# Raw blocks of the output projection's weight sums in idle buffers, and the T1 splits of a Strassen product behind the last head, in a one-core attention and recurrence trunk

## The chip, the cores and the metric

The kernel runs on one core of a Trainium2 chip. The metric is the device time of one execution in microseconds (us). The engines are PE (matrix products; PEld is its weight loading), DVE (vector), ACT (scalar), POOL (GpSimd) and SP, which here only issues transfers.

## The reference

1024 tokens of width 1024 go through two layers. Each has a mixer and a SwiGLU channel mixer, both behind an RMS norm that is shifted and scaled by a conditioning vector (adaLN). Layer 0 mixes by forgetting attention, layer 1 by gated linear attention (GLA), here a recurrence of four heads over eight blocks of 128 tokens:

```python
for i in range(DEPTH):
    mod = c_act @ ada_w[i] + ada_b[i]
    sh1, sc1, g1, sh2, sc2, g2 = jnp.split(mod, N_MOD, axis=-1)
    h = modulate(rms_norm(x, norm1_g[i]), sh1, sc1)
    ...                                   # y: attention (i = 0) or GLA (i = 1)
    x = x + g1[:, None, :] * y
    h = modulate(rms_norm(x, norm2_g[i]), sh2, sc2)
    x = x + g2[:, None, :] * swiglu(h, ffn_w_in[i], ffn_w_out[i])
return rms_norm(x, final_g)

# GLA, per head: state S, decay alpha, q, k, v, gate r
o = o_intra + o_inter                     # A (lower triangle) times v, and q_in times the state before
o = o * lax.rsqrt(jnp.mean(o * o, axis=-1, keepdims=True) + EPS)
o = (o * g_o * silu(r)) ; y = o @ w_out
```

## The kernel before

**Arithmetic.** Every fp32 product is three matrix products of halves. A `split` makes the halves: ACT casts the value to the high part (L174), DVE subtracts it from the value (L175) for the low part. `mm3` issues the three products (L305 to L307). Weights come raw by SP into a ring `wr` of three slots (s16, s17, s18), are split by ACT (L242) and by POOL and DVE (L246), and go on into the ring `ws`.

**Order.** The program is written as generators that are interleaved (`weave`), and each engine's order is then fixed by a scheduler. `tc.issue_after(i)` and `behind_all()` add an order without a wait: what stands under them comes behind instruction i on its engine. `split_after` holds, for each engine, the instruction behind which weight splits and everything under `behind_all()` go.

**The GLA layer** lies at 1280 to 1672 us of the profile. Per head: the k and q projections (`gk`, `gq`), the intra product masked by `atz` and split as `ahl`, the state products `kv`, the state `Sf` and its split `S_t`, the output `go`, its norm (`junk` on ACT, `gss` on DVE and POOL), `on_t` on DVE, its transpose `ogt` on PE and the gate product into `gs` (L2128). `gs` lies in a ring `gsr` of two slots (s47 and s31) and is stored to `og_d` behind each head but the last. Behind a head's recurrence `gv_body` makes the next head's v (`gvt`, slots s48, s49, s53 and s25). Beside all of this `ada1` makes the second channel mixer's conditioning from 64 KB pieces of `ada_w` (`ad`, L442 to load, L505 on DVE), which SP loads in between.

**The output projection** is a Strassen product with seven terms (B11, T1, T2, T3, T4, B21, B22). On the weight side the blocks a11, a12, a21, a22 of `gla_w_out` are added up on POOL by `ow_sums(g)`, for one of four column groups per head, and stored to DRAM as `ow` 5, 7, 6 and 3. On the activation side, with a = `og_t[j]` and c = `og_t[4 + j]` and their halves 0 and 1, T1 = a0 − a1, T2 = c0 − T1 and T3 = c0 − a0. For j = 0 and 1 T2 and T3 are made early; for j = 2 and 3, made of the third and fourth heads, they are made in `out_blocks`, during the last head. Each is split into a `goT` or `goB` tile (`goT23` is T2 for j = 3). The four accumulators `oc0` to `oc3` take B11, T2 and T3 in turn; between them `out_add` (x on DVE, L2302) reads each into the residual, and PE can't go on to the next term in that bank before.

**The channel mixers** (`ffn`, both layers) work in four groups i of two residual tiles each. Behind the last part of a group five additions (on POOL for the first three groups, on DVE for the fourth) and four gate products on DVE finish it.

Of the kernel before, what the change touches and what calls it, by code (L numbers as in the profile page):

```python
# [16 lines left out]
P = 128  # L17
# [36 lines left out]
def trunk(ctx, tc, x, c, ada_w, ada_b, norm1_g, norm2_g, ffn_w_in, ffn_w_out,  # L54
# [910 lines left out]

    def ow_sums(g):

        raw = [wr([P, 2, 4, P], F32, f"pw{g}") for _ in range(2)]
        for i in range(2):
            for j in range(2):  # L970
                nc.sync.dma_start(raw[i][:, j], ow_src(g, (i, j)))
        (a11, a12), (a21, a22) = ((r[:, 0], r[:, 1]) for r in raw)
        yield
        nc.gpsimd.tensor_add(a22, a21, a22)
        yield
        nc.gpsimd.tensor_sub(a21, a11, a21)
        yield
        nc.gpsimd.tensor_sub(a11, a22, a11)
        yield
        nc.gpsimd.tensor_sub(a12, a12, a11)  # L980
        for nm_, r in ((5, a22), (7, a21), (6, a11), (3, a12)):
            d = ow_d[(nm_, g)] = tc.dram_tile([P, 4, P], F32, name=f"ow{nm_}{g}")
            nc.sync.dma_start(d, r)

    OW = [(nm_, g) for nm_ in (1, 6, 7, 5, 3, 2, 4) for g in range(4)]
# [486 lines left out]
    def ffn(l, oh, xs, slots, nm, mid, norm_end, each=None, blocks=None):  # L1472
# [289 lines left out]

        hp, xr, zs, ends = {}, {}, {}, deque()

# [55 lines left out]
        for c_ in range(OC):  # L1820
# [3 lines left out]
            for i in range(4):  # L1824
# [6 lines left out]
                def p_(j):  # L1831
                    ps = prod(feed.next(), o[c_][ONAMES[j]])
                    if last:
                        advance(i + 1 if j else i)
                        if i == 3:
                            advance(8)
                        if j == 2:
                            load_xr(i)
                    elif i < 3:
                        advance(NSP * (7 * i + j + 1) // 21)  # L1840
                    elif j:
                        advance(min(NSP + 3 * j, 7 * OD))
                    return ps
# [23 lines left out]
                fins = [lambda: V.tensor_add(Y1, Y1, Z1), lambda: V.tensor_add(Y4, Y4, Z1),  # L1867
                        lambda: V.tensor_sub(Y2, Y4, Y2), lambda: V.tensor_add(Y4, Y4, Z5),
                        lambda: V.tensor_sub(Y3, Y4, Y3)]
                gates_ = [lambda a=a, hf=hf, v_=v_: gated(a, hf, v_)  # L1870
                          for (a, hf), v_ in (((0, 0), Y1), ((1, 0), Y2), ((1, 1), Y4), ((0, 1), Y3))]
                if i < 3:
                    for f in fins + gates_:
                        f()
                else:
                    ends.extend([fins[0], gates_[0], fins[1], fins[2], gates_[1], None, fins[3], None, fins[4], None,
                                 gates_[2], None, gates_[3]])
# [118 lines left out]

    def gv_body(h, wv, tp):

        ps = pj([P, 2, 256], F32, f"gv{h}{tp}")
        for i in range(2):  # L2000
            run(proj_tok(ps[:, i, :], wv, h1, 2 * tp + i))
        ada1(5.1)
        v = vr([P, 2, 2, 256], FR, f"gvt{h}{tp}")
        split(v[:, 0], v[:, 1], ps)
# [40 lines left out]

    def head_front(h, b16, t2, ei, nmid):


        wk = feed.next()
        sums = ow_sums(h)  # L2050
        next(sums)
        kin = Pair(kir([P, S], FR, f"kih{h}"), kir([P, S], FR, f"kil{h}"))
        for hf in range(2):
# [4 lines left out]
            ada1(5.1)  # L2058
            next(sums)
            y = yv()  # L2060
# [8 lines left out]
        for hf in range(2):  # L2069
# [9 lines left out]
        return kin, qt  # L2079

    def head_back(h, kin, qt, t2, dec, vt, gs, need):
# [53 lines left out]
        for g in range(2):  # L2135
# [6 lines left out]
            for half in range(2):  # L2142
# [19 lines left out]
                for i2 in range(2):  # L2162
                    nc.vector.tensor_scalar(on_t[:, half, i2], o[:, i2, :], sst[:, i2:i2 + 1], None, op0=ALU.mult)
                yield 0.01
            yield from og_out(g)
# [21 lines left out]
    vt = []  # L2187
# [120 lines left out]
    def out_blocks(views):  # L2308
# [9 lines left out]
        for j in (2, 3):  # L2318
            a, c_ = og_t[j], og_t[4 + j]
            nc.gpsimd.tensor_sub(a[:, h1_], a[:, h0_], a[:, h1_])  # L2320
            ob_split("T1", j, a[:, h1_])
            nc.vector.tensor_sub(a[:, h1_], c_[:, h0_], a[:, h1_])
# [139 lines left out]
```

## Time and profile before

| | us |
|---|---|
| time, median of 3 runs (lowest to highest) | 2371.12 (2369.95 to 2371.66) |
| the profiled execution's own time | 2371.09 |
| its span in the trace | 2369.4 |
| PE busy | 2343.2 |
| DVE busy | 1787.3 |
| ACT busy | 1121.9 |
| POOL busy | 1104.7 |

All times within the execution are counted from the start of the span. Busy time is how long an engine worked on its instructions; an engine's idle time costs something only where PE then waits. A row of the timeline gives start, length, engine, line, operation, output and inputs, shape and count, and in brackets the idle time ahead of it and what ended it.

### The profile page before, as it was taken

Reading aid. Unit: us, or ns where it says so; the run is one execution under the profiler, and the core shown is the slowest. Engines: PE = TensorE matmul, PEld = TensorE weight load, DVE = VectorE, ACT = ScalarE, POOL = GpSimd, SP = SyncE. Lnnn points to the kernel's source line nnn. Section 1 sums busy time; section 2 is a strip of 40 time slices with the busy share of each in tenths; the row PEclk is TensorE's granted clock in tenths of the full one; section 3 lists DMA queues with packets and bytes.
Section 4 is the critical chain, followed back from the end, with each engine's and each line's share of the span. In section 5 each row is a group of like instructions: output and inputs, shape, how many; then the busy total and the mean of one; then the engine's idle time right before and its main releaser. Section 6 shows DMA issues by size and latency. Waiting matters only on the chain.

```text
span 2369.4 us, 35786 instructions
## 1 busy us (share of the span) xinstructions
PE 2343.2 (99%) x12208; PEld 1993.9 (84%) x12208; DVE 1787.3 (75%) x2994; ACT 1121.9 (47%) x2186; POOL 1104.7 (47%) x995
## 2 busy tenths in 40 slices
PE   8999999999999999999999999999999999999999
PEld 7888888888888888888888899887888888888888
DVE  6577787886688888876788665668787777875787
ACT  6556566665443333345325644344444333345326
POOL 1334444533445665653363432245356665643262
PEclk9999999999999999999999999999999999999999
DMA  8423333332435555457665453454434544457664
GB/s 259 148 77 114 105 121 94 121 126 98 142 103 168 187 165 168 163 195 256 227 210 165 132 148 110 118 185 161 138 106 163 178 147 151 147 200 257 226 201 150
DMA packets 349998, 375.00 MB, mean 158 GB/s; under 512 B 25756, under 2 KB 287032, under 8 KB 349816
## 3 DMA queue, kind: packets, MB, share of 16 engines
q1 hardware_dynamic: 349816, 372.72, 47.9%
q8 instruction: 96, 1.57, 0.3%
q14 instruction: 86, 0.70, 0.1%
HBM read 275.56 MB, written 97.06 MB: 157 GB/s over the span
## 4 chain that ended last, share of the span: by engine, by line
PE 83%; DVE 7%; DMA 3%; issue 2%; POOL 2%; ACT 2%; SPq 1%; DVEq 0%; POOLq 0%; ACTq 0%
PE p_b L305 15%; PE p_b L307 15%; PE p_b L306 15%; PE o_b L1305 2%; PE t_b L1291 2%; PE qk_b L305 2%; PE qk_b L306 2%; PE qk_b L307 2%; PE vps_b L307 1%; PE vps_b L305 1%; PE vps_b L306 1%; PE s_b L1259 1%; PE s_b L1260 1%; PE gr_b L305 1%; PE gr_b L306 1%
## 5 line engine op out<-in xcount | busy, mean ns | idle before, releaser
L175 DVE TENSOR_TENSOR o_s<-xv_s,o_s 128x512 fp32r<-128x512 f32 (+1 forms) x376 | 322.9, 863 | 57.3 <-ACT o_s L174 57.0
L174 ACT CAST o_s<-xv_s 128x512 fp32r<-128x512 f32 (+1 forms) x376 | 216.6, 587 | 297.3 <-PE p_b L307 249.3
L307 PE MATMUL p_b<-B,o_s 128*128 128x512 f32 x608 | 236.0, 389 | 0.0
L306 PE MATMUL p_b<-B,o_s 128*128 128x512 f32 x608 | 235.9, 389 | 0.0
L305 PE MATMUL p_b<-B,o_s 128*128 128x512 f32 x608 | 235.4, 390 | 0.0
L918 POOL TENSOR_TENSOR ex_s<-xv_s,xv_s 128x512 f32<-128x512 f32 (+1 forms) x64 | 90.8, 1419 | 284.2 <-DMA xv_s<-in_ffn_w_in_dram 118.0
L1271 POOL TENSOR_SCALAR lp_s<-lp_s,st 128x128 f32<-128x128 f32 (+7 forms) x128 | 98.0, 769 | 246.6 <-DVE st L1270 230.4
L305 PE MATMUL p_b<-T,o_s 128*128 128x512 f32 x480 | 186.9, 389 | 0.0
L306 PE MATMUL p_b<-T,o_s 128*128 128x512 f32 x480 | 186.8, 389 | 0.0
L307 PE MATMUL p_b<-T,o_s 128*128 128x512 f32 x480 | 181.2, 389 | 0.0
L307 PEld LDWEIGHTS p_b<-B,o_s 128*128 128x128 f32 x608 | 114.1, 188 | 23.9
L305 PEld LDWEIGHTS p_b<-B,o_s 128*128 128x128 f32 x608 | 114.1, 188 | 23.7 <-DVE x L1636 0.2
L306 PEld LDWEIGHTS p_b<-B,o_s 128*128 128x128 f32 x608 | 114.1, 188 | 23.5
L1269 ACT ACTIVATE lp_s<-lp_s,st 128x128 f32<-128x128 f32 (+7 forms) x128 | 99.4, 777 | 58.5 <-DVE st L1265 57.2
L246 POOL TENSOR_TENSOR w_l_s<-w__s,w_h_s 128x256 fp32r<-128x256 f32 x90 | 71.7, 824 | 100.1 <-ACT w_h_s L242 69.2
L920 POOL TENSOR_TENSOR xv_s<-ex_s,xv_s 128x512 f32<-128x512 f32 (+1 forms) x64 | 87.1, 1362 | 63.3 <-DVE o_s L175 61.1
L174 ACT CAST pt_s<-t_b 128x512 fp32r<-128x512 f32 (+1 forms) x160 | 79.7, 547 | 72.6 <-PE t_b L1291 72.0
L1636 DVE TENSOR_TENSOR ex_s<-ex_s,p_b 128x512 f32<-128x512 f32 x140 | 93.6, 680 | 20.7 <-PE p_b L307 20.6
L175 DVE TENSOR_TENSOR pt_s<-t_b,pt_s 128x512 fp32r<-128x512 f32 (+1 forms) x160 | 96.2, 630 | 15.9 <-ACT pt_s L174 15.4
L307 PEld LDWEIGHTS p_b<-T,o_s 128*128 128x128 f32 x480 | 90.1, 188 | 18.7
L306 PEld LDWEIGHTS p_b<-T,o_s 128*128 128x128 f32 x480 | 90.1, 188 | 18.6
L305 PEld LDWEIGHTS p_b<-T,o_s 128*128 128x128 f32 x480 | 90.1, 188 | 18.6
(1803 smaller groups left out, 7438.0 us busy)
## 6 DMA issues: line engine op xcount, KB each, us to landing
xv_s<-in_ffn_w_in_dram SPq DMA_DIRECT2D x176, 256.0 KB, 3.2
hid_B<-x SPq DMA_DIRECT2D x70, 512.0 KB, 3.0
ad_s<-in_ada_w_dram SPq DMA_DIRECT2D x384, 64.0 KB, 2.3
hid_T<-x SPq DMA_DIRECT2D x36, 512.0 KB, 2.9
xv_s<-in_ffn_w_out_dram SPq DMA_DIRECT2D x96, 192.0 KB, 4.8
ada_s<-in_ada_w_dram SPq DMA_DIRECT2D x96, 128.0 KB, 2.8
xv_s<-in_ffn_w_out_dram SPq DMA_DIRECT2D x40, 256.0 KB, 2.9
T2o<-hid_T SPq DMA_DIRECT2D x18, 512.0 KB, 8.3
```

The source lines that it names most:

```text
L174: nc.scalar.copy(hi, src)
L175: nc.vector.tensor_sub(lo, src, hi.bitcast(F32))
L246: (nc.gpsimd if i < 3 else nc.vector).tensor_sub(lo[:, cs], rw[:, cs], hi[:, cs].bitcast(F32))
L305: nc.tensor.matmul(ps, ah, bh, start=start, stop=False, skip_group_check=chain)
L306: nc.tensor.matmul(ps, ah, bl, start=False, stop=False, skip_group_check=chain)
L307: nc.tensor.matmul(ps, al, bh, start=False, stop=stop, skip_group_check=chain)
L918: nc.gpsimd.tensor_add(s1, a21, a22)
L920: nc.gpsimd.tensor_sub(a11, s1, a11)
L1269: nc.scalar.activation(lp, lp, AF.Exp, bias=mcur, scale=-1.0, accum_out=st[:, qi, 2:3])
L1271: nc.gpsimd.tensor_scalar(lp, lp, st[:, qi, 3:4], 1.0, op0=ALU.mult, op1=ALU.mult)
L1291: nc.tensor.transpose(tp[:, i, :], lps[qi][:, psl(2 * b + jj)], ident)
L1636: nc.vector.tensor_add(d, d if src is None else dest(G, src), ps)
```

## The change

**Weight sums.** `ow_sums` takes its raw blocks from a ring that is handed in instead of from `wr`: for the first head from `qr` (slots of the q tiles, not in use yet), and for the others from `gsr`, the two slots that the head before has just stored to `og_d`. It is started earlier: ahead of the first head, or in `gv_body` of the head before. Each raw block comes by one load of 512 KB instead of two, and the sums go back by two stores of 512 KB instead of four of 256 KB.

**Last head.** T3 is made first (on POOL), T2 = T3 + a1 behind it (on DVE), and T1 as c0 − T2, later. T1's splits, and the other splits under `behind_all()`, now go behind `on_last`, the last ACT and DVE instructions that made `on_t`.

**Channel mixers.** The third group's additions and gates are collected in `pend` and called two at a time behind the products of the fourth group, and the residual of the fourth group is loaded two products later.

```diff
-    def ow_sums(g):
-        raw = [wr([P, 2, 4, P], F32, f"pw{g}") for _ in range(2)]
+    def ow_sums(g, ring):
+        raw = [ring([P, 2, 4, P], F32, f"pw{g}") for _ in range(2)]
         for i in range(2):
-            for j in range(2):
-                nc.sync.dma_start(raw[i][:, j], ow_src(g, (i, j)))
+            nc.sync.dma_start(raw[i].rearrange("p j k m -> p (j k) m"),
+                              gla_w_out[0][:, psl(2 * g + i)].rearrange("(k p) m -> p k m", p=P))
...
-        for nm_, r in ((5, a22), (7, a21), (6, a11), (3, a12)):
-            d = ow_d[(nm_, g)] = tc.dram_tile([P, 4, P], F32, name=f"ow{nm_}{g}")
+        for nms, r in (((7, 5), raw[1]), ((6, 3), raw[0])):
+            d = tc.dram_tile([P, 2, 4, P], F32, name=f"ow{g}{nms[0]}")
             nc.sync.dma_start(d, r)
+            ow_d.update({(nm_, g): d[:, j] for j, nm_ in enumerate(nms)})
...
                         if i == 3:
                             advance(8)
-                        if j == 2:
+                            for _ in range(2):
+                                if pend:
+                                    pend.popleft()()
+                        if j == (2 if i < 3 else 4):
                             load_xr(i)
...
-                if i < 3:
+                if i < 2:
                     for f in fins + gates_:
                         f()
+                elif i == 2:
+                    pend.extend(fins + gates_)
                 else:
+                    while pend:
+                        pend.popleft()()
...
-    def gv_body(h, wv, tp):
+    def gv_body(h, wv, tp, sums):
...
         ada1(5.1)
+        next(sums, None)
         v = vr([P, 2, 2, 256], FR, f"gvt{h}{tp}")
...
-        sums = ow_sums(h)
-        next(sums)
...
+                on_last.update((e, last_of(e)) for e in "AD")
                 yield 0.01
             yield from og_out(g)
...
+    qr.q.rotate(-2)
+    sums = ow_sums(0, qr)
+    next(sums)
...
-        kin, qt = head_front(h, b16, t2, ei, nmid)
+        kin, qt = head_front(h, b16, t2, ei, nmid, sums)
+        run(sums)
...
-            vt = [gv_body(h + 1, wv, tp) for tp in range(4)]
+            sums = ow_sums(h + 1, gsr)
+            vt = [gv_body(h + 1, wv, tp, sums) for tp in range(4)]
...
             a, c_ = og_t[j], og_t[4 + j]
-            nc.gpsimd.tensor_sub(a[:, h1_], a[:, h0_], a[:, h1_])
-            ob_split("T1", j, a[:, h1_])
-            nc.vector.tensor_sub(a[:, h1_], c_[:, h0_], a[:, h1_])
+            nc.gpsimd.tensor_sub(a[:, h0_], c_[:, h0_], a[:, h0_])
+            nc.vector.tensor_add(a[:, h1_], a[:, h0_], a[:, h1_])
             ob_split("T2", j, a[:, h1_])
-            nc.gpsimd.tensor_sub(a[:, h0_], c_[:, h0_], a[:, h0_])
             ob_split("T3", j, a[:, h0_])
-        split_after.update((e, last_of(e)) for e in "AD")
+        split_after.update(on_last)
...
             with behind_all():
                 ob_split("T1", j, a[:, h1_])
+        for j in (2, 3):
+            a = og_t[j]
+            with behind_all():
+                nc.vector.tensor_sub(a[:, h0_], og_t[4 + j][:, h0_], a[:, h1_])
+                ob_split("T1", j, a[:, h0_])
```

The order of the program shows the first part best on SP. In the first head of before, from the load of the second raw block to the second half of the v weight of columns 1280 on (`wv1280`); `pw0` are the raw blocks, `ow` the stores of the sums, each `ad` row four loads:

```order
L971 DMA pw0_s18_84_13355<-in_gla_w_out_dram 128x4x128 x2
L442 DMA ad_s39_12918<-in_ada_w_dram 32x2x256 x4
L442 DMA ad_s40_12919<-in_ada_w_dram 32x2x256 x4
L227 DMA wv1280_0_s16_85_13448<-in_gla_w_in_dram 128x4x256
L983 DMA ow50_13538<-pw0_s18_84_13355 128x512
L983 DMA ow70_13540<-pw0_s18_84_13355 128x512
L983 DMA ow60_13542<-pw0_s17_83_13354 128x512
L983 DMA ow30_13544<-pw0_s17_83_13354 128x512
L442 DMA ad_s39_12918<-in_ada_w_dram 32x2x256 x4
L442 DMA ad_s40_12919<-in_ada_w_dram 32x2x256 x4
L442 DMA ad_s39_12918<-in_ada_w_dram 32x2x256 x4
L227 DMA wv1280_4_s17_86_13561<-in_gla_w_in_dram 128x4x256
```

and of after, from the load of the k weight `w0` to the same place:

```order
L227 DMA w0__s18_81_13097<-in_gla_w_in_dram 128x8x128
L970 DMA pw0_s27_2_13345<-in_gla_w_out_dram 128x8x128
L227 DMA w2176__s16_82_13348<-in_gla_w_in_dram 128x8x128
L970 DMA pw0_s34_1_13344<-in_gla_w_out_dram 128x8x128
L983 DMA ow07_13536<-pw0_s27_2_13345 128x1024
L983 DMA ow06_13538<-pw0_s34_1_13344 128x1024
L227 DMA wv1280_0_s17_83_13446<-in_gla_w_in_dram 128x4x256
L442 DMA ad_s39_12918<-in_ada_w_dram 32x2x256 x4
L442 DMA ad_s40_12919<-in_ada_w_dram 32x2x256 x4
L442 DMA ad_s39_12918<-in_ada_w_dram 32x2x256 x4
L227 DMA wv1280_4_s18_84_13555<-in_gla_w_in_dram 128x4x256
```

The second half of the v weight took the slot of a raw block (s17) and stood behind its stores; now it takes s18, of which `w0` was split, and the raw blocks (s27, s34) are loaded and stored ahead of both halves.

In the last head of before DVE's order from the third `on_t` to the x row of the third accumulator was (`go310` is the third output block of the head, `S_t<-Sf36` the last state split):

```order
L2163 TENSOR_SCALAR on_t_12928<-go310_b5_15_16316,gss310_16317 128x256 x2
L175 TENSOR_TENSOR goT33_16477<-og3_s33_16430,goT33_16477 128x512
L175 TENSOR_TENSOR goT10_16481<-og0_s50_16432,goT10_16481 128x512
L2302 SCALAR_TENSOR_TENSOR x1_2_16450<-oc1_16489,modc_165,x1_2_16450 128x512
L175 TENSOR_TENSOR goT11_16485<-og1_s51_16434,goT11_16485 128x512
L175 TENSOR_TENSOR goB221_16651<-og5_s25_16649,goB221_16651 128x512
L175 TENSOR_TENSOR goB211_16654<-og5_s25_16649,goB211_16654 128x512
L175 TENSOR_TENSOR S_t_12927<-Sf36_16365,S_t_12927 128x256
L2302 SCALAR_TENSOR_TENSOR x1_4_16452<-oc2_16490,modc_165,x1_4_16452 128x512
```

and of after, from the same `on_t`:

```order
L2172 TENSOR_SCALAR on_t_12928<-go310_b5_15_16292,gss310_16293 128x256 x2
L2336 TENSOR_TENSOR og3_s33_16406<-og3_s33_16406 128x512
L2124 SCALAR_TENSOR_TENSOR Sf36_16341<-Sf35_16311,dec3_15603,kv36_b4_28_16337 128x256
L175 TENSOR_TENSOR goT33_16445<-og3_s33_16406,goT33_16445 128x512
L175 TENSOR_TENSOR goT23_16442<-og3_s33_16406,goT23_16442 128x512
L2317 SCALAR_TENSOR_TENSOR x1_2_16426<-oc1_16465,modc_165,x1_2_16426 128x512
L175 TENSOR_TENSOR S_t_12927<-Sf36_16341,S_t_12927 128x256
```

The T1 splits of j = 0 and 1 and two B splits stood between the `on_t` of `go310` and the last state split, the T1 splits of j = 2 and 3 some ten rows ahead of these; now the split of T3 and T2 for j = 3 stands there, with the addition for T2 (`og3`, which reads what POOL made).

Where these went is the stretch from the last `on_t` to the second read of `oc0`. Of before, again on DVE:

```order
L175 TENSOR_TENSOR goT41_16659<-og5_s25_16649,goT41_16659 128x512
L2160 TENSOR_SCALAR gss311_16379<-gss311_16379 128x2
L175 TENSOR_TENSOR goB222_16730<-gs30_s47_7_16064,goB222_16730 128x512
L2163 TENSOR_SCALAR on_t_12928<-go311_b6_16_16378,gss311_16379 128x256 x2
L2302 SCALAR_TENSOR_TENSOR x1_0_16448<-oc0_16488,modc_165,x1_0_16448 128x512
```

and of after:

```order
L2172 TENSOR_SCALAR on_t_12928<-go311_b6_16_16354,gss311_16355 128x256 x2
L175 TENSOR_TENSOR goT10_16449<-og0_s50_16408,goT10_16449 128x512
L175 TENSOR_TENSOR goT11_16453<-og1_s51_16410,goT11_16453 128x512
L2349 TENSOR_TENSOR og2_s37_16404<-gs30_s47_13_16040,og2_s37_16404 128x512
L2349 TENSOR_TENSOR og3_s33_16406<-gs31_s31_14_16041,og3_s33_16406 128x512
L175 TENSOR_TENSOR goB221_16627<-og5_s25_16625,goB221_16627 128x512
L175 TENSOR_TENSOR goB211_16630<-og5_s25_16625,goB211_16630 128x512
L175 TENSOR_TENSOR goB222_16706<-gs30_s47_13_16040,goB222_16706 128x512
L175 TENSOR_TENSOR goT12_16457<-og2_s37_16404,goT12_16457 128x512
L175 TENSOR_TENSOR goT13_16461<-og3_s33_16406,goT13_16461 128x512
L2317 SCALAR_TENSOR_TENSOR x1_0_16424<-oc0_16464,modc_165,x1_0_16424 128x512
```

Nothing stood between the last `on_t` and that read; now nine operations do: the T1 splits of all four j, the two subtractions that make T1 for j = 2 and 3 (`og2`, `og3`), and three B splits.

In the channel mixers the third group's additions, gates and loads have the same places on POOL, DVE and SP in both orders, in both layers.

More of the change, by code (lines that the diff above doesn't have):

```diff
@@ L1761, in part @@
                 yield
-        hp, xr, zs, ends = {}, {}, {}, deque()
+        hp, xr, zs, ends, pend = {}, {}, {}, deque(), deque()
         def last_part():
@@ L1866, in gated @@
                                                    op0=ALU.mult, op1=ALU.add)
-                fins = [lambda: V.tensor_add(Y1, Y1, Z1), lambda: V.tensor_add(Y4, Y4, Z1),
-                        lambda: V.tensor_sub(Y2, Y4, Y2), lambda: V.tensor_add(Y4, Y4, Z5),
-                        lambda: V.tensor_sub(Y3, Y4, Y3)]
+                fins = [lambda f=f, a=a: f(*a) for f, a in (
+                    (V.tensor_add, (Y1, Y1, Z1)), (V.tensor_add, (Y4, Y4, Z1)), (V.tensor_sub, (Y2, Y4, Y2)),
+                    (V.tensor_add, (Y4, Y4, Z5)), (V.tensor_sub, (Y3, Y4, Y3)))]
                 gates_ = [lambda a=a, hf=hf, v_=v_: gated(a, hf, v_)
                           for (a, hf), v_ in (((0, 0), Y1), ((1, 0), Y2), ((1, 1), Y4), ((0, 1), Y3))]
-                if i < 3:
+                if i < 2:
                     for f in fins + gates_:
                         f()
-                else:
+                elif i == 2:
+                    pend.extend(fins + gates_)
+                else:
+                    while pend:
+                        pend.popleft()()
                     ends.extend([fins[0], gates_[0], fins[1], fins[2], gates_[1], None, fins[3], None, fins[4], None,
@@ L2044, in gate_body, with head_front @@
         return b16, t2, ei, (dec, nmid)
-    def head_front(h, b16, t2, ei, nmid):
+    def head_front(h, b16, t2, ei, nmid, sums):
         wk = feed.next()
-        sums = ow_sums(h)
-        next(sums)
         kin = Pair(kir([P, S], FR, f"kih{h}"), kir([P, S], FR, f"kil{h}"))
@@ L2058, in head_front @@
             ada1(5.1)
-            next(sums)
+            next(sums, None)
             y = yv()
@@ L2079, in head_front @@
         return kin, qt
+    on_last = {}
     def head_back(h, kin, qt, t2, dec, vt, gs, need):
```

## Prediction

> **What bounds the kernel now.** I read the page's totals first, then busy time by stage, then PE's waits in the stages that the change touches, then the timelines around those waits. The totals:
>
> ```profile
> span 2369.4 us, 35786 instructions
> PE 2343.2 (99%) x12208; PEld 1993.9 (84%) x12208; DVE 1787.3 (75%) x2994; ACT 1121.9 (47%) x2186; POOL 1104.7 (47%) x995
> ```
>
> PE is the bound; it lacks 26 us of the span, so only its waits can be won. The stage table (window, its length, then busy PE, PEld, DVE, ACT, POOL with counts, granted clock, DMA share, GB/s) says where they lie. The recurrence runs from 1280 to 1672:
>
> ```profile
> 1280.00:1400.00 120.00, 118.17 (x758) 107.00 (x757) 87.87 (x154) 71.51 (x162) 53.91 (x58) 1.00 0.48 143
> 1400.00:1480.00 80.00, 79.92 (x490) 71.02 (x490) 47.87 (x91) 36.37 (x85) 22.84 (x26) 1.00 0.41 121
> 1480.00:1565.00 85.00, 82.19 (x504) 72.72 (x504) 53.12 (x101) 36.46 (x85) 25.18 (x27) 1.00 0.46 139
> 1565.00:1616.00 51.00, 51.00 (x276) 43.90 (x274) 29.03 (x48) 21.71 (x48) 17.12 (x15) 1.00 0.52 175
> 1616.00:1672.00 56.00, 52.71 (x251) 42.99 (x250) 50.73 (x64) 27.30 (x57) 39.84 (x29) 1.00 0.45 146
> ```
>
> Window minus PE gives 1.83, 0.08, 2.81, 0 and 3.29: 8.0 us of waiting in the whole stage, or 0.34% of the kernel. The granted clock is 1.00 in all five, so no speed is to be had there. From 1616 DVE is busy 50.73 of 56.00 us. What PE waited for in 1280 to 1672 (total, times, longest):
>
> ```profile
> PE go_b L306 <- DVE S_t L175: 2.8, 2, 2.4
> PE go_b L305 <- ACT ahl_s L174: 1.9, 2, 1.5
> PE gk_b L305 <- DVE gvt_s L175: 1.0, 1, 1.0
> PE ogt_b L2125 <- DVE on_t L2163: 0.8, 1, 0.8
> PE go_b L305 <- ACT junk L2159: 0.7, 1, 0.7
> PE gr_b L305 <- DVE t_s L2062: 0.5, 1, 0.5
> PE kdt_b L2089 <- DVE kdl_s L175: 0.2, 1, 0.2
> ```
>
> These seven groups hold 7.9 of the 8.0 us. What a measurement of this kernel can tell from no change is about 0.2%, or 4.7 us: more than half of all these waits must go before the gain shows.
>
> **The weight sums' buffers.** In the first head SP's rows (start, length, operation, count) are
>
> ```profile
> 1338.36 0.53 SPq L227 DMA_DIRECT2D wv_s<-in_gla_w_in_dram  x1
> 1338.99 3.01 SPq L983 DMA_DIRECT2D ow<-pw_s  x4
> 1343.62 8.65 SPq L442 DMA_DIRECT2D ad_s<-in_ada_w_dram  x12
> 1352.32 1.92 SPq L227 DMA_DIRECT2D wv_s<-in_gla_w_in_dram  x1
> ```
>
> The second half of the v weight takes the slot of a sum's raw block, so it leaves only at 1352.32, behind the four stores and twelve adaLN loads. It lands late, and PE pays:
>
> ```profile
> 1358.05 1.15 ACT L242 CAST wv_4h_s<-wv_s 128x512 fp32r<-128x512 f32 x2 [4.06 <-DMA wv_s<-in_gla_w_in_dram]
> 1360.44 0.62 ACT L174 CAST ahl_s<-atz_s 128x512 fp32r<-128x512 f32 x1 [0.73 <-DVE atz_s L2099]
> 1361.12 0.39 PE L305 MATMUL go_b<-gvt_s,ahl_s 128*128 128x256 f32 x1 [1.52 <-ACT ahl_s L174]
> ```
>
> ACT stood 4.06 us for that weight, in front of the cast for which PE then stood 1.52 us. After the change the raw blocks lie elsewhere. Counted from the load of `w0`, twelve adaLN loads stand ahead of this weight instead of twenty-eight, and two stores instead of four. In SP's time (8.65 us for twelve loads, 0.72 each) sixteen loads are 11 us, well over ACT's 4.06, and the wait goes: −1.4 (bounds −1.5 if nothing else is late, +0.7 if one wait of the mean size of these, 0.73, comes on top).
>
> In the third head the same queue shows
>
> ```profile
> 1476.26 0.38 SPq L227 DMA_DIRECT2D wv_s<-in_gla_w_in_dram  x1
> 1477.29 5.45 SPq L442 DMA_DIRECT2D ad_s<-in_ada_w_dram  x8
> 1483.03 0.87 DVE L505 SCALAR_TENSOR_TENSOR ad_s<-ad_s,c 128x256 f32<-128x256 f32 x1 [5.73 <-DMA ad_s<-in_ada_w_dram]
> 1483.82 0.68 DVE L175 TENSOR_TENSOR gvt_s<-gv_b,gvt_s 128x512 fp32r<-128x512 f32 x1
> 1471.41 0.32 SPq L983 DMA_DIRECT2D ow<-pw_s  x1
> ```
>
> SP had nothing to issue from 1471.73 to 1476.26: the v weight needs the slot that the store of 1471.41 reads. Eight adaLN loads and DVE's adaLN product queued behind it, and behind that the split for which PE stood 1.0 us. In the new order that weight load takes a slot that no sum has used, and comes ahead of the sum's loads: −0.97, with 0 as the other bound, since the adaLN loads then queue behind the new waits (the sum's loads go into the buffers that `og_d` was just stored from, and wait on SP for that store to land).
>
> The other waits of the second to fourth heads (0.5 for `t_s`, 0.2 for `kdl_s`, 0.4 of the second `ahl_s` wait, 0.7 for `junk`) stand behind DVE and ACT work that waits for weights in the same way, though less plainly: I take −0.7 of the first three (bounds 0 and −1.1) and −0.5 of `junk` (0 and −0.75). POOL's sums are the same four per head, now on blocks that nothing else waits for. As every engine is laid out anew here, I add one new wait of mean size, rounded up: +0.8.
>
> **The last head.** Before the last recurrence product PE stood longest, as DVE came late:
>
> ```profile
> 1636.82 0.30 PE L2125 MATMUL ogt_b<-ident,on_t 128*128 128x128 f32 x1 [0.76 <-DVE on_t L2163]
> 1642.45 1.48 DVE L175 TENSOR_TENSOR S_t<-Sf,S_t 128x256 fp32r<-128x256 f32 x1
> 1643.98 0.39 PE L306 MATMUL go_b<-S_t,gq31h_s 128*128 128x256 f32 x1 [2.44 <-DVE S_t L175]
> 1648.14 0.88 DVE L2163 TENSOR_SCALAR on_t<-go_b,gss 128x256 f32<-128x256 f32 x2 [0.59 <-POOL gss L2161]
> 1648.94 0.74 DVE L2302 SCALAR_TENSOR_TENSOR x<-oc,modc,x 128x512 f32<-128x512 f32 x1
> 1652.07 0.39 PE L305 MATMUL oc<-goT,ow_s 128*128 128x512 f32 x1
> ```
>
> The last row is the first T3 product; it needs the bank that the x row at 1648.94 reads. Without the 3.3 us of waits of this window PE would be there at 1648.8. What the work on DVE and POOL costs in this stretch (busy us and mean ns of one):
>
> ```profile
> L175 DVE TENSOR_TENSOR goT<-og_s,goT 128x512 fp32r<-128x512 f32 x9 | 8.5, 962 | 0.0
> L175 DVE TENSOR_TENSOR goB<-og_s,goB 128x512 fp32r<-128x512 f32 x7 | 8.3, 1223 | 0.0
> L2322 DVE TENSOR_TENSOR og_s<-gs_s,og_s 128x512 f32<-128x512 f32 x2 | 3.1, 1527 | 0.0
> L175 DVE TENSOR_TENSOR goB<-gs_s,goB 128x512 fp32r<-128x512 f32 x1 | 0.7, 681 | 0.0
> L2320 POOL TENSOR_TENSOR og_s<-og_s 128x512 f32<-128x512 f32 x2 | 3.4, 1712 | 1.2 <-DVE goB L175 1.2
> 1628.93 1.78 DVE L2322 TENSOR_TENSOR og_s<-gs_s,og_s 128x512 f32<-128x512 f32 x1
> ```
>
> Four goT and two goB splits move from ahead of the last S_t to behind the last `on_t`: 4 × 0.96 + 2 × 1.22 = 6.3 us, less 0.5 of overlap, so S_t is ready at 1643.9 − 5.8 = 1638.1. The two T2 additions that stand ahead of it in place of the L2322 subtractions wait for POOL's subtraction first; I take that as paid by the two L2320 subtractions (1.7 each) that POOL no longer does beside DVE. PE, no longer held, wants S_t at about 1637: 48 T2 products now follow the last S_t product ahead of 1648.8, at 0.22 each (719.55 us for 3264 in a row further down). So that wait falls to about 1, and the `on_t` wait goes. But the x row now stands behind all of it. From the S_t product (1644.2) to the end of the last `on_t` (1649.0) lie 4.8 us, 0.7 of them DVE's other work; with the product at 1638.4 and 4.1 behind it, `on_t` ends at 1642.5. Behind it stand eight more operations and the one goB of 0.68: by the mean rows (4 goT, 2 goB, 2 og subtractions, less 0.08 overlap each) 9.3 us, and the x row of 0.74: it ends at 1652.5, and PE is 0.4 later than in before. At 0.68 each (the row that stands alone) it ends at 1648.6, and nearly all of 3.3 is won: −2.9. At the longest row, 1.78 each, it ends at 1657.4: +5.4. I lie near the mean rows and a little below them, since DVE has less POOL work beside it: x ends at 1651.5, **−0.6**.
>
> A rule of the Trainium skill speaks against the change here. "SBUF — State Buffer", section "Who interferes with whom", says that a DVE instruction with two SBUF inputs contends with a GpSimd instruction that reads SBUF, by a lock held for the whole instruction, and that the loser fully blocks. By it each of the eight could cost its own 0.68 and a whole POOL operation, about 2.0 in all, which I estimate at F = +8.5 and 2376.8 for the kernel. The means of 0.96 and 1.22 agree that two-input splits are held up, but only partly so.
>
> **The third group's mixers.** In the order of the program the additions, gates and loads of that group stand where they stood, on POOL, DVE and SP, in both layers, since the scheduler had already drawn them there. Should they move after all, there is the cover of the products: before 1280 and after 1672 PE hardly waits:
>
> ```profile
> 560.00:1280.00 720.00, 719.55 (x3264) 596.82 (x3263) 573.52 (x800) 290.03 (x525) 364.38 (x268) 1.00 0.51 173
> 1672.00:2370.00 698.00, 691.36 (x3203) 577.33 (x3201) 531.34 (x728) 291.97 (x525) 354.37 (x247) 1.00 0.51 174
> ```
>
> 0.45 us of waiting in the first, and in the second nearly all of the 6.6 at the end of the span. So 0; a gain is excluded by the 0.45, a loss by the unchanged rows.
>
> **The sum.** −1.4 − 0.97 − 0.7 − 0.5 − 0.6 + 0.8 = −3.4 against the profiled execution, whose time is 2371.09 us (span 2369.4 and 1.7 around it). That is the median of the runs shown, 2371.12, within 0.03. The forecast is 2367.7.
>
> **The rivals.** *All waits of the stage go.* For it: every long one of them ends in a weight that came late or a split that stood in front. Against it: removing one wait usually lets the next-latest engine show. −1.5 − 0.3 − 0.97 − 1.1 − 0.75 − 2.9 = −7.5: 2363.6.
>
> *The x row is late (slower).* The eight operations behind `on_t` run beside POOL's T4 subtractions and weight splits and take the longest row each. PE then stands 8.7 us before T3 instead of the 3.3 that it stood in this head: 2371.1 + 5.4 − 2.8 for the other terms = 2373.7. It decides against the change once the x row ends more than 6.1 us after 1648.8, that is at 1654.9, which is 1.4 us for each of the eight. For it: goB has a mean of 1.22 and single rows reach 1.78. Against it: goT has 0.96 and a lone one 0.68.
>
> *The waits only move.* The new loads of raw blocks wait for the `og_d` store, and with them the adaLN loads behind; the third head and the later ones win nothing: 2371.1 − 1.4 = 2369.7. This is also about what comes out if the change does not free the queue as it says.
>
> **How the numbers follow.** Forecast 0.42 (own range 2365.8 to 2369.7, a fifth of it below 2366.4), all waits go 0.28, x row late 0.18, waits only move 0.12. Faster by over 0.2% means below 2366.4, slower above 2375.9. Faster: 0.42 × 0.2 + 0.28 = 0.36. Slower: just over half of the late x row, where the single-row price is exceeded: 0.10. The rest is 0.54. The range goes from the first rival's 2363.3 to 2374.5, a little above the price of the second; what lies outside is about a third of the first and over half of the second, 2 in 10.
>
> **What would show it.** ACT's cast of the v weight in the first head has no wait of 4 us, and PE's wait of 1.52 is gone; SP has no hole of 4.5 us ahead of the third head's v weight; PE's wait for S_t is below 1 us; the first T3 product stands at an x row that ends at about 1651.5 on this clock. I am wrong if PE's idle time in the last head exceeds 3.3 us, if new waits of over 1 us appear in the second to fourth heads, or if the mixers' stages, before 1280 and after 1672, differ by over 0.5 us.

## The result, and the profile after

| | before | after |
|---|---|---|
| time, median of 9 runs each (lowest to highest), us | 2370.40 (2368.07 to 2371.66) | 2363.66 (2362.25 to 2367.52) |
| the profiled execution: time and span, us | 2371.09, 2369.4 | 2362.25, 2360.5 |
| ratio (95% interval) | | 0.9971 (0.9962 to 0.9980) |

The change makes the kernel faster by 0.29%; the medians lie 6.7 us apart. A second comparison gave 0.9969 (0.9958 to 0.9981). The totals and the five stages of the recurrence, of after (in the stages: window, its length, then busy PE, PEld, DVE, ACT, POOL with counts, granted clock, DMA share, GB/s):

```profile
PE 2339.7 (99%) x12208; PEld 1992.7 (84%) x12208; DVE 1791.0 (76%) x2996; ACT 1122.5 (48%) x2186; POOL 1101.5 (47%) x993
1280.00:1400.00 120.00, 120.00 (x775) 109.43 (x774) 88.35 (x157) 73.73 (x167) 50.14 (x57) 1.00 0.46 138
1400.00:1480.00 80.00, 79.65 (x491) 70.79 (x490) 48.52 (x92) 34.21 (x82) 20.45 (x24) 1.00 0.43 122
1480.00:1565.00 85.00, 85.00 (x526) 76.18 (x525) 54.43 (x104) 38.54 (x90) 27.68 (x32) 1.00 0.46 135
1565.00:1616.00 51.00, 51.00 (x267) 43.34 (x266) 34.12 (x51) 23.09 (x52) 22.81 (x18) 1.00 0.66 218
1616.00:1672.00 56.00, 55.53 (x259) 45.60 (x259) 46.87 (x64) 28.12 (x55) 38.65 (x28) 1.00 0.42 136
```

Window minus PE (the idle time of PE) is now 0, 0.35, 0, 0 and 0.47: 0.8 us of waiting where before had 8.0. All of PE's waits in 1280 to 1672 of after that the view lists (total, times, longest):

```profile
PE oc L305 <- DVE x L2317: 0.5, 1, 0.5
PE kdt_b L2098 <- DVE kdl_s L175: 0.2, 1, 0.2
```

None of the seven groups of before is left but a rest for `kdl_s`. On SP, in the first head, the second half of the v weight leaves at 1336.43 instead of 1352.32:

```profile
1326.49 9.84 SPq L442 DMA_DIRECT2D ad_s<-in_ada_w_dram  x12
1336.43 0.53 SPq L227 DMA_DIRECT2D wv_s<-in_gla_w_in_dram  x1
```

In the third head SP still has a hole, and a longer one than before. The first half of the v weight is issued by 1459.3; then SP has nothing to issue until a block that is stored to `og_d` is ready, and the second half leaves 11 us later than in before (1476.26):

```profile
1470.23 0.34 SPq L2294 DMA_DIRECT2D og_d<-gs_s  x1
...
1487.25 0.53 SPq L227 DMA_DIRECT2D wv_s<-in_gla_w_in_dram  x1
```

PE doesn't wait there all the same: the eight adaLN loads that stood behind the hole of before leave at 1471.62 instead of 1477.29, and DVE stands 2.01 us for them instead of 5.73.

DVE's rows of the last head, from the last state split to the second x row, the one new wait:

```profile
1629.33 0.41 DVE L175 TENSOR_TENSOR S_t<-Sf,S_t 128x256 fp32r<-128x256 f32 x1
...
1632.55 0.88 DVE L2172 TENSOR_SCALAR on_t<-go_b,gss 128x256 f32<-128x256 f32 x2 [0.81 <-POOL gss L2170]
1633.35 1.60 DVE L175 TENSOR_TENSOR goT<-og_s,goT 128x512 fp32r<-128x512 f32 x2
1634.87 2.38 DVE L2349 TENSOR_TENSOR og_s<-gs_s,og_s 128x512 f32<-128x512 f32 x2
1637.17 1.28 DVE L175 TENSOR_TENSOR goB<-og_s,goB 128x512 fp32r<-128x512 f32 x2
1638.37 0.68 DVE L175 TENSOR_TENSOR goB<-gs_s,goB 128x512 fp32r<-128x512 f32 x1
1638.98 2.38 DVE L175 TENSOR_TENSOR goT<-og_s,goT 128x512 fp32r<-128x512 f32 x2
1641.28 0.74 DVE L2317 SCALAR_TENSOR_TENSOR x<-oc,modc,x 128x512 f32<-128x512 f32 x1
```

The nine operations behind the last `on_t` take 8.0 us (1633.35 to 1641.36). Six of them take 0.68 and follow each other every 0.6; the first takes 1.00, and one in the pair at 1634.87 and one in the pair at 1638.98 take 1.78. The three long ones have a POOL operation beside them, for the first two these:

```profile
1632.50 1.30 POOL L1006 TENSOR_TENSOR ow_s<-wa_s,ow_s 128x512 fp32r<-128x512 f32 x1
1635.09 1.61 POOL L2370 TENSOR_TENSOR og_s<-og_s,og_s 128x512 f32<-128x512 f32 x1 [1.29 <-DVE goT L175]
```

### The profile page after: what moved, and what is told of

The parts are those of the page before. It is cut to its first block, busy times and chain, and to the rows that moved or that the text cites. A ratio compares the mean times of both kernels' runs of the same rounds, so it can differ in the third digit from the quotient of the medians.

```text
span 2360.5 us, 35758 instructions
## 1 busy us (share of the span) xinstructions
PE 2339.7 (99%) x12208; PEld 1992.7 (84%) x12208; DVE 1791.0 (76%) x2996; ACT 1122.5 (48%) x2186; POOL 1101.5 (47%) x993
```

## The experiments

The runs of one kernel scatter by 0.1 to 0.2% to either side (before again, against itself: 0.9999, 0.9990 to 1.0008), so where the time went is read from the traces, by two stretches of PE. "Heads" runs from the first v product to the first output product, "output" from there to the second channel mixer. Each row is one trace, in us:

| kernel | heads | output | ratio to before (95% interval) |
|---|---|---|---|
| before | 331.2 | 86.5 | |
| before_again | 328.7 | 86.5 | 0.9999 (0.9990 to 1.0008) |
| transfers_only | 328.0 | 86.7 | 1.0006 (0.9997 to 1.0015) |
| buffers_only | 335.2 | 83.7 | 1.0010 (1.0001 to 1.0019) |
| sums_only | 324.9 | 85.9 | 0.9996 (0.9988 to 1.0005) |
| sums_again | 327.0 | 85.9 | 0.9985 (0.9976 to 0.9994) |
| order_only | 328.4 | 84.9 | 0.9987 (0.9978 to 0.9995) |
| behind_only | 329.5 | 89.7 | 1.0002 (0.9993 to 1.0011) |
| last_only | 329.0 | 84.5 | 0.9988 (0.9980 to 0.9997) |
| after | 325.1 | 83.2 | 0.9971 (0.9962 to 0.9980) |
| after_again | 325.9 | 83.2 | 0.9969 (0.9958 to 0.9981) |
| t1_later | 328.0 | 82.6 | 0.9974 (0.9965 to 0.9984) |
| pool_beside | 327.2 | 88.1 | 0.9996 (0.9986 to 1.0005) |
| pool_quiet | 326.6 | 82.4 | 0.9965 (0.9954 to 0.9977) |

The output stretch comes back within 0.1 us wherever a kernel was traced twice. The heads do not: the same program differs by 2.5 us (before) and 2.1 (the sums alone). In buffers_only the border lies elsewhere: 13 products of the recurrence that follow the first output product in all the other kernels come ahead of it. So only the sum of its two stretches compares, 418.9 us, where before has 417.7 and 415.2 and the sums' change alone 410.8 and 412.9. The mixers' part was not run by itself; by operation and tile the order of every engine up to 1240 us and from 1680 us on is the same in the traces of before and after.

**before_again and after_again**: both kernels once more, unchanged.

> Before once more, for a second trace and as a comparison of the kernel with itself: ratio 1.000 within 0.001. The question is which of PE's waits belong to the program. Theory A: the four long ones (1.5 for the first head's ahl, 1.0 for the third head's gvt split, 0.8 for on_t and 2.4 for S_t in the last head) come again within 0.3 us. Theory B: the waits ahead of the last head hang on when loads land and differ by 1 us and more from one execution to the next; only the last head's two come again.

> After once more: ratio 0.9971 within its interval (0.996 to 0.998). Theory A: PE waits under 1 us in the first four heads and 0.5 us for the second x row, as in its first trace. Theory B: the heads show other waits of 0.3 to 0.8 us, up to 2 us in all, as two of its relatives did (a wait of 0.8 for h1l near 1314, three of 0.2 to 0.4 near 1424, one of 0.7 near 1507), and the last head is the same again.

PE's waits in 1280 to 1672 of before, in the second trace:

```profile
PE go_b L306 <- DVE S_t L175: 2.7, 2, 2.4
PE ogt_b L2125 <- DVE on_t L2163: 1.1, 2, 0.8
PE go_b L305 <- ACT junk L2159: 0.8, 1, 0.8
PE go_b L305 <- ACT ahl_s L174: 0.6, 2, 0.4
...
PE gk_b L305 <- DVE gvt_s L175: 0.3, 1, 0.3
```

For before theory B holds in the main: the 1.52 for `ahl_s` was now 0.37, and the 0.97 for the v split 0.31. The last head's waits (2.4 and 0.8) came again to 0.05 us, and so, against it, did the one for `junk` near 1555. After_again has three waits (0.5 for x, 0.4 for `gq10l_s`, 0.2 for `kdl_s`), which decides for neither theory.

**sums_only and sums_again**: the change without the last head's and the mixers' parts, run twice. Against after:

```diff
-            nc.gpsimd.tensor_sub(a[:, h0_], c_[:, h0_], a[:, h0_])
-            nc.vector.tensor_add(a[:, h1_], a[:, h0_], a[:, h1_])
+            nc.gpsimd.tensor_sub(a[:, h1_], a[:, h0_], a[:, h1_])
+            ob_split("T1", j, a[:, h1_])
+            nc.vector.tensor_sub(a[:, h1_], c_[:, h0_], a[:, h1_])
...
-        split_after.update(on_last)
+        split_after.update((e, last_of(e)) for e in "AD")
```

> The weight sums in idle buffers alone; the last head and the mixers as in before. Theory 1 (each wait of PE costs its row): the waits of the first to fourth heads ahead of the output products go, 4.7 us of rows less some 0.4 that stay, so 4.4 us faster, ratio 0.9981, and the last head still waits 3.3 us. Theory 2 (a wait costs 0.26 us more than its row, since the row starts at the modelled end of the matmul, 0.16 after the next could have issued, and the second matmul behind a wait issues 0.10 late): 9 waits, 6.1 us faster, ratio 0.9974. Rival (the gain needs the last head's change too, since SP's order there moves with it): under 2 us faster.

> The weight sums' change alone once more, since its first trace showed 4.1 us less and its runs only 0.1 per cent. If the trace was typical: stretch of 325 to 326 us, ratio 0.9983. If the runs were: stretch of 327 to 328, ratio 0.9993. In the last head again about 0.6 us less than in before, by another split of the same waits.

The two ratios, 0.9996 and 0.9985, overlap only narrowly; their mean, some 2 us, is less than either theory's and the first trace's (4.1). Five traces with the sums in the weight ring whose last head doesn't matter here (before twice, last_only, order_only, behind_only) have 329.4 us in the heads on average, and the seven with the sums' whole change 326.4: 3.0 us less. The gain there doesn't need the last head's change, as the rival had it: 324.9 and 327.0 without, 325.1 to 328.0 with it. The wait for `ahl_s` in the first head (0.4 to 1.5 in each of the five) and the one for `junk` (0.75) are in none of the seven. In their place some of the seven show a wait of 0.8 for `h1l` near 1314, of 0.4 for `gq10` near 1424, and of 0.4 to 0.7 for `t_s` near 1507.

The sums alone change the last head too, though nothing of its code: both traces have no wait for S_t left, but waits of 1.0 for `on_t` and of 1.4 to 1.5 for two x rows, and the output stretch is 0.6 us shorter.

**transfers_only and buffers_only**: the two halves of that part. The first, against before, merges the transfers and leaves the raw blocks in `wr`; the second takes the idle buffers and the early start, with two loads a block and four stores as in before:

```diff
 # transfers_only, against before
-            for j in range(2):
-                nc.sync.dma_start(raw[i][:, j], ow_src(g, (i, j)))
+            nc.sync.dma_start(raw[i].rearrange("p j k m -> p (j k) m"), ...)
...
 # buffers_only, against before
-        raw = [wr([P, 2, 4, P], F32, f"pw{g}") for _ in range(2)]
+        raw = [ring([P, 2, 4, P], F32, f"pw{g}") for _ in range(2)]
...
```

> Before with the raw blocks still in the weight ring, but loaded by one transfer each instead of two and stored by two instead of four. Measured by the stretch from the first v product to the first output product: it took 328.4 to 331.2 us in the five traces so far with the sums in the weight ring, and 324.9 to 328.0 in the five with idle buffers. If SP's issue time (16 transfers fewer, some 0.7 us each) is what counts: 326 or less, ratio 0.9985. If the slots count: 328 to 331 as in before, ratio 1.000.

> Before with the raw blocks in the idle buffers and loaded early as in after, but by two transfers of 256 KB each, and stored by four. If the slots count: 325 to 328 us for the same stretch, no weight load waits for a store, ratio 0.9985. If SP's issue time counts: 328 or more, ratio 1.000.

Neither theory holds alone. Merged transfers by themselves gain nothing that the runs show; their 328.0 us in the heads lie 0.4 below the lowest of the five traces above, within the scatter. The idle buffers by themselves gain nothing either (418.9 us for both stretches). Two of PE's three longest waits there, and the rows behind them in the third head (SP, then DVE):

```profile
PE gr_b L305 <- DVE t_s L2061: 2.2, 1, 2.2
...
PE kv_b L307 <- DVE kdl_s L175: 1.5, 1, 1.5
...
1490.02 1.73 SPq L983 DMA_DIRECT2D ow<-pw_s  x2
1494.80 2.48 SPq L442 DMA_DIRECT2D ad_s<-in_ada_w_dram  x4
1497.38 1.00 SPq L983 DMA_DIRECT2D ow<-pw_s  x2
...
1499.58 5.83 SPq L442 DMA_DIRECT2D ad_s<-in_ada_w_dram  x8
...
1505.92 0.79 DVE L505 SCALAR_TENSOR_TENSOR ad_s<-ad_s,c 128x256 f32<-128x256 f32 x1 [5.78 <-DMA ad_s<-in_ada_w_dram]
1507.50 0.68 DVE L175 TENSOR_TENSOR kdl_s<-kdt_b,kdh_s 128x512 fp32r<-128x512 f32 x1
```

SP spends its time with four stores in two lots and a hole of 3.1 us at 1491.75; eight adaLN loads come after, DVE stands 5.78 us for them until 1505.92, and the splits that PE wants stand behind. The same place in after, on nearly the same clock (the first v product starts at 1290.7 and 1290.8), has two stores and the loads 5.6 us earlier:

```profile
1489.48 2.47 SPq L442 DMA_DIRECT2D ad_s<-in_ada_w_dram  x4
1492.05 1.29 SPq L983 DMA_DIRECT2D ow<-pw_s  x2
...
1494.02 11.35 SPq L442 DMA_DIRECT2D ad_s<-in_ada_w_dram  x14
```

DVE stands for adaLN loads there too, 5.49 us, but only until 1500.56, and PE doesn't wait. So the gain needs both halves. As I read the rows, the buffers free the weight loads, and the merged transfers keep the queue from being late with the adaLN loads; that rests on one trace of each half. The ratio of buffers_only (1.0010) lies above that of the sums' whole change both times, though its interval overlaps the first of those.

**last_only, order_only, behind_only**: the last head's part alone, and its two halves. Order_only makes T3 first, T2 from it and T1 late, but puts the splits where before had them; behind_only has the new place of the splits and the old order of the T blocks:

```diff
 # last_only, against after: the sums as in before
-        next(sums, None)
-            sums = ow_sums(h + 1, gsr)
+        sums = ow_sums(h)
...
 # order_only, against last_only
-        split_after.update(on_last)
+        split_after.update((e, last_of(e)) for e in "AD")
 # behind_only, against before
-        split_after.update((e, last_of(e)) for e in "AD")
+        split_after.update(on_last)
...
```

> The last head alone (T3 first, T2 from it, T1 of j = 2 and 3 late, splits behind the last on_t); the raw blocks of the sums stay in the weight ring. Theory 1: PE's waits for S_t (2.4) and on_t (0.8) go and one of about 0.5 for the second x row comes: 2.8 us faster, ratio 0.9988. Theory 2 (0.26 more for each wait): 3.3 us faster, ratio 0.9986. Rival, the prediction's mean rows: the x row ends 2.7 us late and 0.6 us are won, ratio 0.9997.

> Before with T3 first, T2 from it and T1 of j = 2 and 3 made last, but the splits still put behind the last T3 split, not behind the last on_t. DVE does as much ahead of the last S_t as in before (six splits and two additions that wait for POOL), so if the place of the splits is what counts PE still waits 2 us or more for S_t, and the kernel is within 1 us of before, ratio 1.000. If the order of the T blocks is what counts (less work on POOL beside DVE), the wait for S_t falls below 1 us and the ratio is 0.9988, as with both.

> Before with the splits put behind the last on_t, but T1, T2, T3 made in the old order, so that the T1 splits of j = 2 and 3 stay ahead of S_t. If the place of the splits is what counts, S_t comes 3 to 4 us earlier, PE's wait for it goes or falls below 0.5, the second x row waits behind seven splits instead of nine operations and PE waits under 1.5 us for it: about 2 us faster, ratio 0.999. If the order of the T blocks counts, PE still waits 2 us for S_t.

PE's waits from 1600 to 1672, of the three in turn:

```profile
PE oc L305 <- DVE x L2305: 1.8, 2, 1.6
```

```profile
PE oc L305 <- DVE x L2305: 0.7, 1, 0.7
PE go_b L306 <- DVE S_t L175: 0.6, 1, 0.6
PE ogt_b L2127 <- DVE on_t L2165: 0.4, 1, 0.4
```

```profile
PE oc L305 <- DVE x L2305: 3.6, 1, 3.6
PE ogt_b L2127 <- DVE on_t L2165: 0.8, 1, 0.8
PE go_b L306 <- DVE S_t L175: 0.4, 1, 0.4
```

Last_only wins 2.0 us of the output stretch (ratio 0.9988): between theory 1 (2.8) and the rival (0.6), since its x rows cost 1.8 us instead of 0.5: the nine operations ahead of the second x row are those of after, in the same order, but take 9.4 us (1634.87 to 1644.32), as POOL holds up four of them and not three. Order_only wins 1.6, and the wait for S_t falls to 0.6: the order counts. (Ahead of that S_t stood four of the six splits, not all as I expected; the T1 splits of j = 2 and 3 came behind it.) Behind_only brings the wait for S_t down to 0.4 as well, so the place frees S_t too, but it loses 3.2 us in the output stretch at the second x row, for a reason that no theory had. (1.6 of these are waits, 4.8 instead of 3.2; for the rest see the last section.) DVE there, in behind_only:

```profile
1648.12 2.96 DVE L175 TENSOR_TENSOR goB<-og_s,goB 128x512 fp32r<-128x512 f32 x2 [3.20 <-ACT goB L174]
```

The scheduler put two more B splits ahead of the x row, of `og4`, whose load had not landed; DVE stood 3.2 us. In after the T1 splits fill that place and the two stand behind the x row. So the order, the place and the sums each take most or all of the wait for S_t; what they are worth lies in the waits that they leave elsewhere.

**t1_later, pool_beside, pool_quiet**: what sets the second x row. All three against after:

```diff
 # t1_later: the last block of the change, inside the T3 products behind the first out_add
+                with tc.issue_after(x_first[0]):
+                    for j in (2, 3): ...            # the subtraction and the T1 split
...
 # pool_beside: six times behind the last norm, into a tile nobody reads
+                        nc.gpsimd.tensor_tensor(idle, ident..., sst..., op=ALU.add)
...
 # pool_quiet: T4 of j = 0 and 1 made on DVE, behind the second x row
-            nc.gpsimd.tensor_sub(a[:, h1_], c_[:, h0_], a[:, h1_])
-            nc.gpsimd.tensor_sub(c_[:, h1_], c_[:, h1_], a[:, h1_])
+                        nc.vector.tensor_sub(a[:, h1_], c_[:, h0_], a[:, h1_])
+                        nc.vector.tensor_sub(c_[:, h1_], c_[:, h1_], a[:, h1_])
```

> After, with the subtractions and splits that make T1 for j = 2 and 3 moved again, behind the second x row of the first accumulator (four of the nine operations that stood ahead of it). If DVE's chain sets that row, PE's wait of 0.47 us for it goes and the first T3 product starts 0.6 us earlier: 2363.0 where after has 2363.7, ratio to before 0.9969. If a POOL operation sets it through the two-input lock, the chain gets shorter by two of the four only, and 0.3 us are left. If the later places make T1 late for its own product, a new wait of up to 1 us shows some 20 us further on.

> After, with six extra POOL additions (128x512 into a scratch tile that nobody reads) strewn behind the last norm on POOL, so that POOL hardly rests while DVE does the nine operations ahead of the second x row. The full lock: each DVE operation with two SBUF inputs waits for one whole POOL operation, 1.8 to 2.0 us instead of 0.68; the nine take 14 to 16 us instead of the 7.9 in after, the x row ends 6 to 8 us later and PE's wait grows from 0.5 to 6 or 8; ratio to before about 1.0000. Partial slowing as the mean rows of before have it (0.96 to 1.22): the nine take 9.3 us, PE waits about 1.9, ratio 0.9977. No contention: unchanged, 0.9971.

> After, with the four POOL subtractions that make T4 for j = 0 and 1 done on DVE behind the second x row instead. Two of them held up DVE operations of the nine to 1.77 us. If POOL operations beside them are the whole excess: all of the nine but the first take 0.68 us, the nine 6 us instead of 8.0, PE's wait of 0.5 for the x row goes, 0.6 us faster than after, ratio 0.9968. If DVE then has too much behind the x row (four operations more), a new wait of up to 1 us shows in the T3 products and nothing is won.

DVE in pool_quiet:

```profile
1635.61 1.60 DVE L175 TENSOR_TENSOR goT<-og_s,goT 128x512 fp32r<-128x512 f32 x2
1637.13 1.28 DVE L2349 TENSOR_TENSOR og_s<-gs_s,og_s 128x512 f32<-128x512 f32 x2
1638.34 1.28 DVE L175 TENSOR_TENSOR goB<-og_s,goB 128x512 fp32r<-128x512 f32 x2
1639.54 0.68 DVE L175 TENSOR_TENSOR goB<-gs_s,goB 128x512 fp32r<-128x512 f32 x1
1640.14 1.28 DVE L175 TENSOR_TENSOR goT<-og_s,goT 128x512 fp32r<-128x512 f32 x2
```

and in pool_beside, with a weight split of POOL in the same stretch:

```profile
1636.54 2.54 DVE L175 TENSOR_TENSOR goT<-og_s,goT 128x512 fp32r<-128x512 f32 x2
1639.00 3.22 DVE L2354 TENSOR_TENSOR og_s<-gs_s,og_s 128x512 f32<-128x512 f32 x2
1642.14 2.13 DVE L175 TENSOR_TENSOR goB<-og_s,goB 128x512 fp32r<-128x512 f32 x2
1644.80 3.42 DVE L175 TENSOR_TENSOR goT<-og_s,goT 128x512 fp32r<-128x512 f32 x2
...
1636.79 1.74 POOL L1006 TENSOR_TENSOR ow_s<-wa_s,ow_s 128x512 fp32r<-128x512 f32 x1
```

The nine operations take 5.8 us with POOL quiet, 8.0 in after, and 11.7 with POOL busy; PE's wait for the x row goes 0, 0.5, 4.1, and the output stretch 82.4, 83.2, 88.1. DVE does the same nine in the same order in all three, so the difference is POOL's work beside them. (Of the last step of the output stretch, 4.9 us, the wait explains 3.7; for the rest see the last section.) With POOL busy 11.7 lies between the full lock (14 to 16) and the mean rows (9.3): six of the nine take 1.5 to 1.8 us and three 0.68 to 0.84, where POOL was idle or about to end. T1_later takes four operations out of the chain and PE's wait goes as well (82.6).

Pool_quiet is the fastest version by its ratio, 0.9965 against 0.9969 and 0.9971 for after, but the intervals overlap; its 0.8 us of the output stretch is shown by its trace alone.

## Why the prediction was right and wrong

The time, 2363.66, lies inside the range, at its lower end. (That end, 2363.3, is 0.3 below the 2363.6 that the rival's own sum gives.) The likeliest case, 2367.7 and within 0.2%, did not come true; the rival did that had all waits of the stage go (2363.6, chance 0.28). That it met the time to 0.1 us is luck: it took 4.6 from the heads and 2.9 from the last head, the traces show 3.0 and 3.3, and the median of before itself came out 0.7 lower than the 2371.1 that it started from.

- **Weight sums.** In the first head the mechanism is as described: the v weight is early, ACT's wait of 4.06 is gone and PE's of 1.52 with it. In the third head it isn't. The second half of the v weight stands behind the sum's loads and not ahead of them, and SP has a hole of 10.9 us (11.3 in after_again) where none of 4.5 was to be. PE's wait of 0.97 went as the adaLN loads left 5.7 us earlier; that wait was 0.31 in before's second trace anyhow. The terms add up to −2.8 with the new wait (−1.4 − 0.97 − 0.7 − 0.5 + 0.8); the traces average −3.0, and new waits of the size allowed for did come. So this part's sum was about right, but only on average: the first trace of after, read alone, would have had it at 6.1, and the runs of the sums alone give 0.9 and 3.6. The bounds for single waits were of little use: they vary by as much themselves.
- **Last head.** This is the term that was mis-sized: −0.6 predicted, −3.3 measured, in two traces of each kernel. On the clock of before (6.5 us later than after's there) the last S_t was ready at 1636.2 instead of 1638.1, `on_t` ended at 1639.9 instead of 1642.5, and the x row at 1648.5 instead of 1651.5. So of the 3.0 us that the x row came earlier than priced, 1.9 were won by S_t, 0.7 between S_t and `on_t`, and only 0.4 in the nine operations and the x row (1.4 against the mean rows). The step that failed took rows of before (means of 0.96, 1.22 and 1.53, and S_t's own split as it stood) for operations that would stand beside other work of POOL. The means mix 0.68 with 1.1 to 1.8, by what POOL did beside each. S_t's own split took 1.48 in before, beside a POOL operation, and 0.41 in after: 1.1 of the 1.9. Order_only keeps four of the six splits and the two T1 subtractions ahead of S_t, with two POOL subtractions less, and its wait for S_t is 0.6 instead of 2.4; what in the new order brings this is not shown. The low bound, −2.9, was the nearer.
- **Whose 3.3 these are.** The last head's part alone takes 2.0 from the output stretch (one trace) and the sums alone 0.6 (two); the two together take 0.7 more than that. In last_only the nine operations cost what the mean rows say (9.4 against 9.3), in after less, with the same code of the last head. How many of them meet a POOL operation the prediction did not work out, so part of the gain over the forecast is luck.
- **The lock.** The Trainium skill's rule ("SBUF — State Buffer", "Who interferes with whom") was set against the means as if they spoke for a partial hold-up. Pool_quiet and pool_beside agree with the rule for a single operation: it takes 0.68 us or waits for the rest of POOL's operation, up to 1.8 in all. What made 2376.8 too high is how often the two meet, not the rule; and by its own terms (eight at 2.0, one at 0.68 and the x row, from 1642.5) the estimate would have been +7.8 and 2376.1.
- **The late x row.** The mechanism exists (4.1 us of waiting in pool_beside, 1.6 in last_only), but not at POOL's load in after.
- **Rows as prices.** The output stretch gained 3.3 where the rows of waits fell by 2.7 (3.2 to 0.5). Theory 2, 0.26 us more for each wait, gives 3.0, which is nearer; as a rule for every wait it is not shown. In the heads the scatter is too wide to tell.
- **Third group's mixers.** Zero, since the order is the same. The sign of being wrong that I set, a difference of over 0.5 us in these stages, was too fine: in the first trace of after PE waits 0.55 us at 1712.46 for `rs` of POOL, in the second it doesn't, and last_only and transfers_only, with the mixers of before, wait 0.47 and 0.31 there.

## What to carry to other kernels

Before you price an operation that moves, look at what the neighbouring engine does at its new place: a mean over a busy stretch is no price in a quiet one, and the operation that it stood in front of may get cheaper too. Take a second trace before you price waits of under a microsecond that hang on loads; those that hang on an engine's order come back to a tenth. When a buffer is freed, ask the issuing queue too, since what it no longer waits for and what it still has to issue decide together.

## What the runs showed of the hardware

PE's idle row understates a wait. In after the first T3 product, by its starts on PE:

```profile
1641.31 0.39 PE L307 MATMUL oc<-goT,ow_s 128*128 128x512 f32 x1
1642.16 0.47 PE L305 MATMUL oc<-goT,ow_s 128*128 128x512 f32 x1 [0.47 <-DVE x L2317]
1642.47 0.40 PE L306 MATMUL oc<-goT,ow_s 128*128 128x512 f32 x1
```

The starts lie 0.85 apart where products of this size start 0.23 apart: 0.62 us lost, where the row says 0.47, since the row counts from the modelled end of a product that takes 0.39. The next one starts 0.08 late as well.

A long wait costs more. In pool_beside, behind PE's wait of 4.14 us (window, then busy times as above, and the granted clock third from the right):

```profile
1649.60:1651.70 2.10, 2.10 (x6) 1.63 (x5) 2.10 (x3) 1.11 (x2) 2.10 (x2) 0.50 0.00 0
```

The clock is 0.50 instead of 1.00, and products of the same size start 0.43 apart instead of 0.23, until 1651.72. That costs some 1.3 us on top of the wait. In behind_only the same shows behind the wait of 3.56 us, from 1653.35 to 1656.7, 1.5 us after PE went on. Behind the 2.44 us of before the clock stayed at 1.00.

A DVE operation with two inputs in SBUF that a POOL operation holds up ends 0.55 us behind it (128x512). In after POOL's row of 1632.50 ends at 1633.80 and DVE's first split at 1634.35; POOL's row of 1635.09 ends at 1636.70 and DVE's second subtraction at 1637.25. So the price is what is left of POOL's operation, and anything from 0.68 to 1.8 us can come of it. POOL pays for it too: in pool_beside its weight split took 1.74 us beside DVE, and 1.28 at 1649.08 in the same trace, where it came first and DVE's split was held up instead.
